# Startup, pooling-group and normalization steps of a one-core hybrid decoder step reordered between ScalarE, VectorE and GpSimd

## The chip, the cores and the metric

The kernel runs on one core of a Trainium2 chip. The metric is the device time in microseconds (us) of one execution, lower is better. Engines are named as in the profile: PE is TensorE (matmul), PEld its weight loads, DVE is VectorE, ACT is ScalarE, POOL is GpSimd and SP is SyncE, which issues most DMAs here.

## The reference

One inference step of one decoder layer on 288 token columns: a prompt of 256 positions and 8 sequences of 4 new tokens. All arithmetic is float32.

```
h    = RMSNorm(x) * g1
proj = h @ w_in + b_in                       # 2048 -> 1024 (a), 1024 (gate), 1024 (z)
u    = a * sigmoid(gate)
c    = silu(LayerNorm(depthwise_causal_conv(u, 31 taps)))
d    = mean of z over the last w positions - z      # w = 2, 4, 8, 16, one w per 256 columns
p    = (d @ pool_w) * pool_scale             # 256x256 for each of the four groups
x   += concat(c, p) @ w_out                  # 2048 -> 2048
x   += relu(RMSNorm(x) * g2 @ w_ff1)^2 @ w_ff2      # 2048 -> 8192 -> 2048
y    = RMSNorm(x) * gf
```

The kernel also returns the newest 30 columns of u and the newest 15 of z as states.

## The kernel before

**Layout.** Channels lie on the 128 partitions and the 288 tokens in the free dimension. Each product of float32 operands is made as three fp32r matmuls of 128x288: the weight's high part times the operand's high part, weight low times operand high, weight high times operand low. So each piece of 128x1024 weights that arrives by DMA in a raw buffer (`wr`, six of them) has to be split into `whi`, a cast on ACT (L274), and `wlo`, a subtraction: on DVE (way "V", L279), on POOL in two halves (way "G", L282), or by ACT and an accumulating DMA (way "D", L276 and L277). There are five buffers each for `whi` and `wlo`. A table `WAYS` gives the ways by stage, in turn.

**Order of the stages.** The first product makes the first two pairs of the input projection (conv channels 0 and 1, four PSUM banks) in eight pairs of k tiles, as the weights and the activations `xT` arrive. Then a written list, `SEQUENCE`, sets the rest of the first half: c2, c3, c4, p3, c5, p2, P3, c6, p1, P2, p0, P1, c7, P0. Here `c` and a number is a conv pair (two banks `ac`, then scaling, gate, 31 taps on ACT, DVE and POOL), small `p` is the input product of a pooling group (`pool_group`) and capital `P` the 256x256 product of that group's differences (`pool_products`, bank `pp`). The numbers in tile names count instances, so `dx3` and `pp3` are the third pooling group to come, whose window is 4 wide, and `ac12` is the product p0, `ac13` the product c7. After that come eight products of w_out with the pooling half, with the LayerNorm's mean, sums and rows between them (`BETWEEN`), eight with the conv half, the feed-forward part in four chunks, and the final norm with the output.

**What sets the order of instructions.** A scheduler writes one fixed order for each engine from priorities (the order in the code, moved by `later`) and from what it takes to be ready. The helper `mm` chains the matmuls of the first half in the order of the code, up to the stage P1: there `chain.clear()` lets the matmuls of P1, c7 and P0 go wherever the scheduler puts them. `issue_after` forces one instruction behind another on its engine's queue. On the chip each queue runs in that fixed order and waits with semaphores.

**A pooling group.** DVE scales the bank into `tz` (L483), ACT adds the bias into `z_all` (L486, L487), POOL makes windowed sums `s` by doubling (L492: two instructions per doubling), divides the sums of the first positions by their own counts (L496, `rcnt`), scales the sums of the new tokens (L499) and makes their difference (L500). DVE makes the difference `d` of the prompt (L497). ACT casts `d` to the high part of `dx` (L502) and DVE makes the low part (L503). Then PE can multiply.

**Start and end.** Nine fp32 matmuls on constants (`warm`, two PE records each) run before data arrives. The first k pair's operand `hx` is made on DVE and ACT from `xT` and the first norm's factors (`vec`). RMSNorm's row factor is applied after the first product, from a sum of squares made meanwhile (`squares`, L418). Row factors come from a square root on ACT, a reciprocal on DVE and one Newton step.

Of the kernel before, what the change touches and what calls it, by code (L numbers as in the profile page):

```python
# [16 lines left out]
P = 128  # L17
D = 2048
# [54 lines left out]
WAYS = {"c2": "GVGV", "c3": "GDGG", "c4": "GDGD", "p3": "GDDG", "c5": "GDGD", "c": "GGGV", "p": "GVVG", "w0": "VV", "w": "GG", "ff": "VV"}  # L73
# [13 lines left out]
def trunk_kernel(ctx: ExitStack, tc: tile.TileContext, io):  # L87
# [119 lines left out]
    def load_table(func, src):  # L207

        return nc.scalar.activation(few[: src.shape[0], :], src, func)

    load_table(AF.Sqrt, ones[:, 0:1])
    warm = ms("warm")
    for j in range(9):
# [17 lines left out]
    def inverse_root(mean, root, y, out):  # L231

        nc.vector.reciprocal(y, root)
        nc.vector.scalar_tensor_tensor(out=root, in0=mean, scalar=EPS, in1=y, op0=ALU.add, op1=ALU.mult)
        nc.vector.scalar_tensor_tensor(out=root, in0=root, scalar=-0.5, in1=y, op0=ALU.mult, op1=ALU.mult)
        nc.vector.scalar_tensor_tensor(out=out, in0=root, scalar=1.5, in1=y, op0=ALU.add, op1=ALU.mult)

    def rsqrt_sums(parts, scale, after=None):
# [4 lines left out]
        pt = pq[:, 0, :]  # L243
        for n, t in enumerate(parts):
            for j in range(3):
                last = mm(pt[:TB, j : j + 1], t[:, j * TB : (j + 1) * TB], ones[:, 0:1], start=n + j == 0, stop=n == len(parts) - 1 and j == 2)
        st = const.tile([TB, 12], F32, name=nm("st"))
        s = [st[:, 3 * j : 3 * j + 3] for j in range(4)]
# [17 lines left out]
    turns = {}  # L266

    def split_part(raw, src, hi, lo, way):
# [9 lines left out]
        elif way == "V":  # L278
            nc.vector.tensor_tensor(lo, raw, f32(hi), op=ALU.subtract)  # L279
# [77 lines left out]
    hx, firsts = [], []  # L357

    def first_split(k0):
# [5 lines left out]
        for k in range(k0, k0 + 2):  # L365
            if k == 0:
                nc.vector.tensor_scalar(hx[k][0], xT[:, k, :], v("norm1_g", k), None, op0=ALU.mult)  # L367
            else:
                nc.scalar.activation(hx[k][0], xT[:, k, :], AF.Copy, scale=v("norm1_g", k))  # L369
        for b in blocks[1:]:  # L370
            nc.scalar.copy(hi[:, b], raw[:, b])
        for b in blocks:
            nc.vector.tensor_tensor(lo[:, b], raw[:, b], f32(hi[:, b]), op=ALU.subtract)
# [37 lines left out]
    def squares():  # L411

        nc.scalar.copy(scratch[:, :, :, 0:1], f32(firsts[2][0])[:, 1, 1, 0:10].rearrange("p (n k t) -> p n k t", n=5, t=1))
        for q in range(8):
# [3 lines left out]
            nc.scalar.activation(dst, xq, AF.Square)  # L418
# [365 lines left out]
```

## Time and profile before

| what | value |
|---|---|
| median of 3 runs | 1084.99 us (1084.27 to 1086.06) |
| the profiled execution: time, span | 1084.57 us, 1082.8 us |
| granted PE clock, mean | 0.997 |
| PE busy | 1071.5 us, 99% |
| DVE busy | 635.4 us, 59% |
| ACT busy | 479.0 us, 44% |
| POOL busy | 173.6 us, 16% |
| DMA | 190.71 MB, mean 176 GB/s |

The span counts from the first to the last thing recorded, and 1.8 us of the execution lie outside it. A matmul's duration (292 ns) overlaps the next one's, so the pace is read from starts. "x4" in a row means that four like instructions stand together, and the start is that of the first. Idle time in brackets stands with what ended it.

### The profile page before, as it was taken

How to read it: one execution, taken by the hardware profiler on the slowest of the kernel's cores; microseconds unless marked ns; L12 is line 12 of the kernel's file. 1: busy time of each engine (PE TensorE's matmuls, PEld its weight loads, DVE VectorE, ACT ScalarE, POOL GpSimd, SP SyncE). 2: the span in 40 equal slices, each digit the busy share in tenths (PEclk: the TensorE clock that was granted, in tenths of full speed). 3: DMA queues.
4: the chain of work that ended last, by engine and by line, in shares of the span. 5: the costliest groups of instructions: out<-in, count | busy, mean ns of one | idle time of the engine just before them, and what ended most of it. 6: DMA issues, size and time to landing. Idle time of an engine off the chain costs nothing.

```text
span 1082.8 us, 19572 instructions
## 1 busy us (share of the span) xinstructions
PE 1071.5 (99%) x8198; PEld 1069.9 (99%) x8198; DVE 635.4 (59%) x818; ACT 479.0 (44%) x585; POOL 173.6 (16%) x180
## 2 busy tenths in 40 slices
PE   9999999999999999999999999999999999999996
PEld 9999999999999999999999999999999999999996
DVE  8899999678655544445544444545544445554553
ACT  8654445475544433334443333444433334444441
POOL 0878979512000000000000000000000000000001
PEclk9999999999999999999999999999999999999998
DMA  9896468545555555555555555555555555555522
GB/s 325 281 273 185 137 196 239 176 152 177 173 164 170 172 166 169 174 164 169 171 168 168 175 165 169 174 167 167 174 165 168 174 169 165 173 166 168 173 78 88
DMA packets 58296, 190.71 MB, mean 176 GB/s; under 512 B 6240, under 2 KB 11232, under 8 KB 58208
## 3 DMA queue, kind: packets, MB, share of 16 engines
q1 hardware_dynamic: 56336, 184.35, 53.9%
q0 software_dynamic: 1008, 3.67, 1.9%
q8 instruction: 64, 1.05, 0.4%
q10 hardware_dynamic: 864, 1.44, 0.4%
q14 instruction: 24, 0.20, 0.1%
HBM read 185.16 MB, written 4.28 MB: 175 GB/s over the span
## 4 chain that ended last, share of the span: by engine, by line
PE 77%; issue 20%; ACT 1%; DVE 0%; DMA 0%; POOL 0%; POOLq 0%
PE ac L305 77%; PE pp L305 1%; DMA wr<-in_w 0%; ACT whi L274 0%; POOL xT L720 0%; ACT n L595 0%; DVE wlo L279 0%; PE pt L305 0%; PE pmean L305 0%; POOLq L770 0%; DVE xT L695 0%; DVE n L592 0%; ACT whi L364 0%; ACT mx L597 0%; DVE hx L367 0%
## 5 line engine op out<-in xcount | busy, mean ns | idle before, releaser
L274 ACT CAST whi<-wr 128x1024 fp32r<-128x1024 f32 (+1 forms) x332 | 348.0, 1049 | 551.4 <-PE ac L305 533.5
L279 DVE TENSOR_TENSOR wlo<-wr,whi 128x1024 fp32r<-128x1024 f32 x288 | 353.1, 1226 | 348.5 <-ACT whi L274 348.5
L305 PE MATMUL ac<-ax,whi 128*128 128x288 f32 x2048 | 351.0, 292 | 0.0
L305 PE MATMUL ac<-fx,whi 128*128 128x288 f32 x2048 | 350.2, 292 | 0.0
L305 PEld LDWEIGHTS ac<-ax,whi 128*128 128x128 f32 x2048 | 296.0, 187 | 0.0
L305 PEld LDWEIGHTS ac<-fx,whi 128*128 128x128 f32 x2048 | 295.6, 187 | 0.0
L305 PE MATMUL ac<-ax,wlo 128*128 128x288 f32 x1024 | 217.4, 292 | 0.0
L305 PE MATMUL ac<-fx,wlo 128*128 128x288 f32 x1024 | 216.4, 292 | 0.0
L305 PEld LDWEIGHTS ac<-ax,wlo 128*128 128x128 f32 x1024 | 162.6, 187 | 0.0
L305 PEld LDWEIGHTS ac<-fx,wlo 128*128 128x128 f32 x1024 | 162.3, 187 | 0.0
L305 PE MATMUL ac<-hx,whi 128*128 128x288 f32 x768 | 131.8, 295 | 1.2 <-DVE hx L367 1.2
L720 POOL TENSOR_TENSOR xT<-xT,rf 128x288 f32<-128x288 f32 x4 | 3.1, 795 | 800.1 <-ACT rf L724 800.1
L305 PEld LDWEIGHTS ac<-hx,whi 128*128 128x128 f32 x768 | 112.1, 190 | 1.4 <-ACT hx L369 1.4
L282 POOL TENSOR_TENSOR wlo<-wr,whi 128x512 fp32r<-128x512 f32 x74 | 100.3, 1410 | 35.3 <-ACT whi L274 34.3
L461 DVE SCALAR_TENSOR_TENSOR pc<-u_all,vec,pc 128x256 f32<-128x256 f32 x232 | 99.5, 483 | 1.9 <-ACT pc L458 0.7
L305 PE MATMUL ac<-hx,wlo 128*128 128x288 f32 x384 | 80.1, 294 | 0.0
L305 PEld LDWEIGHTS ac<-hx,wlo 128*128 128x128 f32 x384 | 61.1, 190 | 0.0
L305 PE MATMUL ac<-dx,whi 128*128 128x288 f32 x256 | 46.0, 296 | 0.0
L305 PE MATMUL ac<-mx,whi 128*128 128x288 f32 x256 | 45.1, 294 | 0.1
L664 DVE SCALAR_TENSOR_TENSOR t<-ac,r 128x576 f32<-128x576 f32 x32 | 24.2, 758 | 25.1 <-PE ac L305 25.1
L305 PEld LDWEIGHTS ac<-dx,whi 128*128 128x128 f32 x256 | 38.0, 188 | 0.2
L305 PEld LDWEIGHTS ac<-mx,whi 128*128 128x128 f32 x256 | 37.5, 188 | 0.6 <-ACT mx L597 0.4
(133 smaller groups left out, 533.6 us busy)
## 6 DMA issues: line engine op xcount, KB each, us to landing
wr<-in_w SPq DMA_DIRECT2D x335, 512.0 KB, 3.8
wlo<-in_w POOLq DMA_DIRECT2D x7, 512.0 KB, 7.7
xT<-in_xT SPq DMA_DIRECT2D x8, 288.0 KB, 7.3
wr<-in_w SPq DMA_DIRECT2D x5, 256.0 KB, 3.6
out_u_out<-u_all SPq DMA_DIRECT2D x1, 1208.0 KB, 9.3
u_all<-in_hist_c SPq DMA_DIRECT2D x8, 136.0 KB, 6.2
out_z_out<-z_all SPq DMA_DIRECT2D x1, 668.0 KB, 9.9
z_all<-in_hist_p SPq DMA_DIRECT2D x4, 152.0 KB, 7.5
```

What stands on the lines that cost most here:

```text
L274: nc.scalar.copy(hi, raw)
L279: nc.vector.tensor_tensor(lo, raw, f32(hi), op=ALU.subtract)
L282: nc.gpsimd.tensor_tensor(lo[:, j : j + 2, :], raw[:, j : j + 2, :], f32(hi[:, j : j + 2, :]), op=ALU.subtract)
L305: last = nc.tensor.matmul(*args, **kw)
L461: nc.vector.scalar_tensor_tensor(out=dst, in0=up[:, w : w + SEQ], scalar=cwv[:, w : w + 1], in1=pc, op0=ALU.mult, op1=ALU.add)
L664: nc.vector.scalar_tensor_tensor(out=t, in0=bk[:, :, :T], scalar=0.0, in1=both(rows2[0]), op0=ALU.max, op1=ALU.mult)
L720: eng.tensor_tensor(xk, xk, r[:, None, :].to_broadcast([P, n, T]), op=ALU.mult)
```

## The change

Six parts.

- **Start.** The DMA of the first norm's factors moves from the front of SP's queue to ACT's queue, behind the first weight block. There are 15 warm matmuls in place of 9. On DVE the first `hx` stands ahead of the first weight split; on ACT both weight blocks of the first pair are cast ahead of the second `hx`. The squares are tied one by one behind the pairs' activations.
- **First row factors.** DVE in place of ACT copies them (`rb`) and scales the four banks at once behind that. The fourth low part of stage c2 (way "L") is made behind this.
- **Inverse roots.** ACT reads the mean square from PSUM with the function Abs_reciprocal_sqrt, and three DVE instructions follow; the reciprocal on DVE, and for the row sums two more instructions, go. This is for the first norm, the LayerNorm, the feed-forward norms and the last norm.
- **Ways of the splits.** c2, c3, c4, c7 and p0 get tables of their own. A way "V" split whose code comes after a pooling group is tied behind that group's DVE difference (`behind_pool`).
- **Pooling groups and conv sums.** POOL's three steps on the first and newest columns stand in the code ahead of DVE's difference. For the last two groups they get a higher priority, as do the scaling and gates of the first two conv pairs and the steps of the LayerNorm. The last additions into the channel sums `sum_c` move to the last conv pair, behind its product `prd`.
- **LayerNorm rows and end.** The rows are spread one k pair earlier; the silu pieces are ordered behind the casts; the first output's parts are (1,1,1,1,2,3,3) tiles in place of (1,1,2,2,3,3).

```diff
-WAYS = {"c2": "GVGV", "c3": "GDGG", "c4": "GDGD", "p3": "GDDG", "c5": "GDGD", "c": "GGGV", "p": "GVVG", "w0": "VV", "w": "GG", "ff": "VV"}
+WAYS = {"c2": "GVGL", "c3": "GVGG", "c4": "GVGD", "p3": "GDDG", "c5": "GDGD", "c7": "GGGG", "c": "GGGV", "p0": "GVGG", "p": "GVVG", "w0": "VV", "w": "GG", "ff": "VV"}
...
             first_weights(k, nc.scalar, slice(0, 1))
+            nc.scalar.dma_start(vec[:, 0:NG], io["vec"][:, 0:NG])
             first_weights(k, nc.sync, slice(1, 2))
-    nc.sync.dma_start(vec[:, 0:NG], io["vec"][:, 0:NG])
...
-    for j in range(9):
+    for j in range(15):
         nc.tensor.matmul(warm[:, 0, 0:P], ones, ones, start=True, stop=True)
...
-    def inverse_root(mean, root, y, out):
-        nc.vector.reciprocal(y, root)
-        nc.vector.scalar_tensor_tensor(out=root, in0=mean, scalar=EPS, in1=y, op0=ALU.add, op1=ALU.mult)
-        nc.vector.scalar_tensor_tensor(out=root, in0=root, scalar=-0.5, in1=y, op0=ALU.mult, op1=ALU.mult)
-        nc.vector.scalar_tensor_tensor(out=out, in0=root, scalar=1.5, in1=y, op0=ALU.add, op1=ALU.mult)
+    def inverse_root(mean, y, t, out, after=None):
+        nc.scalar.activation(y, mean, AF.Abs_reciprocal_sqrt, bias=eps[: y.shape[0], :])
+        if after is not None:
+            load_table(after, y[:, 0:1])
+        nc.vector.scalar_tensor_tensor(out=t, in0=mean, scalar=EPS, in1=y, op0=ALU.add, op1=ALU.mult)
+        nc.vector.scalar_tensor_tensor(out=t, in0=t, scalar=-0.5, in1=y, op0=ALU.mult, op1=ALU.mult)
+        nc.vector.scalar_tensor_tensor(out=out, in0=t, scalar=1.5, in1=y, op0=ALU.add, op1=ALU.mult)
...
-        nc.vector.tensor_scalar(s[0], pt[:TB, 0:3], scale * DC, EPS, op0=ALU.mult, op1=ALU.add)
-        nc.scalar.activation(s[1], s[0], AF.Sqrt)
-        if after is not None:
-            load_table(after, s[1][:, 0:1])
-        nc.vector.reciprocal(s[2], s[1])
-        nc.vector.tensor_tensor(s[3], s[2], s[2], op=ALU.mult)
-        nc.vector.scalar_tensor_tensor(out=s[3], in0=s[3], scalar=-0.5, in1=s[0], op0=ALU.mult, op1=ALU.mult)
-        nc.vector.scalar_tensor_tensor(out=s[2], in0=s[3], scalar=1.5, in1=s[2], op0=ALU.add, op1=ALU.mult)
-        return s[2], pq[:, 1, :T], last
+        inverse_root(mean, st[:, 0:3], t, st[:, 4:7], after=after)
+        return st[:, 4:7], pq[:, 1, :T], last
...
         elif way == "V":
-            nc.vector.tensor_tensor(lo, raw, f32(hi), op=ALU.subtract)
+            with tc.issue_after(behind_pool[0]) if behind_pool else nullcontext():
+                nc.vector.tensor_tensor(lo, raw, f32(hi), op=ALU.subtract)
+        elif way == "L":
+            late.append((lo, raw, f32(hi)))
...
-            if i == N8 - 2:
-                for part in (sum_c[:, 1, :], c):
-                    nc.gpsimd.tensor_tensor(sum_c[:, 0, :], sum_c[:, 0, :], part, op=ALU.add)
+            if i == N8 - 1:
+                for part in (sum_c[:, 1, :], cs[i // 2][:, 0, :]):
+                    with tc.issue_after(multiplied.ins):
+                        nc.gpsimd.tensor_tensor(sum_c[:, 0, :], sum_c[:, 0, :], part, op=ALU.add)
...
-        first_sums = s[:, :, PH : PH + w - 1]
-        nc.gpsimd.tensor_tensor(first_sums, first_sums, rcnt[:, None, w - 2 : 2 * w - 3].to_broadcast([P, 2, w - 1]), op=ALU.mult)
-        nc.vector.scalar_tensor_tensor(out=d[:, :, 0:SEQ], in0=s[:, :, PH:ZO], scalar=1.0 / w, in1=z[:, :, PH:ZO], op0=ALU.mult, op1=ALU.subtract)
-        news = [x[:, :, ZO:ZL].rearrange("p m (b t) -> p m b t", t=ZS)[:, :, :, PH:] for x in (s, z)]
-        nc.gpsimd.tensor_scalar(news[0], news[0], 1.0 / w, None, op0=ALU.mult)
-        nc.gpsimd.tensor_tensor(d[:, :, SEQ:T].rearrange("p m (b t) -> p m b t", t=NS), news[0], news[1], op=ALU.subtract)
-        dh, dl = act2("dx", tag="p", bufs=4)
-        nc.scalar.copy(dh, d)
-        nc.vector.tensor_tensor(dl, d, f32(dh), op=ALU.subtract)
+        with later(-LATER if g < 2 else 0):
+            first_sums = s[:, :, PH : PH + w - 1]
+            nc.gpsimd.tensor_tensor(first_sums, first_sums, rcnt[:, None, w - 2 : 2 * w - 3].to_broadcast([P, 2, w - 1]), op=ALU.mult)
+            news = [x[:, :, ZO:ZL].rearrange("p m (b t) -> p m b t", t=ZS)[:, :, :, PH:] for x in (s, z)]
+            nc.gpsimd.tensor_scalar(news[0], news[0], 1.0 / w, None, op0=ALU.mult)
+            nc.gpsimd.tensor_tensor(d[:, :, SEQ:T].rearrange("p m (b t) -> p m b t", t=NS), news[0], news[1], op=ALU.subtract)
+            pooled = nc.vector.scalar_tensor_tensor(out=d[:, :, 0:SEQ], in0=s[:, :, PH:ZO], scalar=1.0 / w, in1=z[:, :, PH:ZO], op0=ALU.mult, op1=ALU.subtract)
+            dh, dl = act2("dx", tag="p", bufs=4)
+            nc.scalar.copy(dh, d)
+            nc.vector.tensor_tensor(dl, d, f32(dh), op=ALU.subtract)
         dd[g] = dh, dl
+        behind_pool[:] = [pooled.ins]
...
-        nc.scalar.copy(rb, pr)
+            nc.vector.tensor_copy(rb, pr)
+            for b in (pair0[1], pair0[0], pair1[1], pair1[0]):
+                scaled = nc.vector.tensor_tensor(b[:, :T], b[:, :T], rb, op=ALU.mult)
+        with tc.issue_after(scaled.ins):
+            nc.vector.tensor_tensor(*late.pop(), op=ALU.subtract)
...
-    BETWEEN = {5: {4: ln_mean}, 6: {6: ln_sums}, 7: {2: ln_rows}}
+    BETWEEN = {5: {4: ln_mean}, 6: {6: ln_sums}, 7: {0: ln_rows}}
...
-    root, first, s_f = [cst[:TB, 2 + 3 * j : 5 + 3 * j] for j in range(3)]
-    nc.scalar.activation(root, sums_f, AF.Sqrt, bias=eps[:TB, :])
-    inverse_root(sums_f, root, first, s_f)
+    s_f = cst[:TB, 6:9]
+    inverse_root(sums_f, cst[:TB, 2:5], ends[:TB, 0, 4:7], s_f)
...
-    finish(nc.vector, rows_f, ((0, 1), (1, 1), (2, 2), (4, 2), (6, 3), (9, 3)))
+    finish(nc.vector, rows_f, ((0, 1), (1, 1), (2, 1), (3, 1), (4, 2), (6, 3), (9, 3)))
```

Three places show what this does to the queues. First PE, from the beginning of product p0 (`ac12`), where the twelve matmuls of the product P2 have just ended; `whi43` and `wlo43` to `whi47` are the weights in their order of arrival, 47 the small pooling block and 48 the first of c7. Before:

```order
L305 MATMUL ac12_1924<-hx2_177,whi43_1897 128x288 x2
L305 MATMUL ac12_1924<-hx2_177,wlo43_1898 128x288 x2
L305 MATMUL ac12_1924<-hx2_177,whi43_1897 128x288 x4
L305 MATMUL ac12_1924<-hx2_177,wlo43_1898 128x288 x2
L305 MATMUL ac12_1924<-hx2_177,whi43_1897 128x288 x2
L305 MATMUL ac12_1924<-hx3_188,whi44_1902 128x288 x2
L305 MATMUL ac12_1924<-hx3_188,wlo44_1903 128x288 x2
L305 MATMUL ac12_1924<-hx3_188,whi44_1902 128x288 x4
```

And after, from the last rows on `whi43`:

```order
L303 MATMUL ac12_1924<-hx2_183,whi43_1896 128x288 x4
L303 MATMUL ac12_1924<-hx2_183,wlo43_1897 128x288 x2
L303 MATMUL ac12_1924<-hx2_183,whi43_1896 128x288 x2
L303 MATMUL ac12_1924<-hx3_194,whi44_1901 128x288 x2
L303 MATMUL ac13_2090<-hx1_172,whi48_2061 128x288 x2
L303 MATMUL pp3_2044<-dx3_1876,whi47_2023 128x288 x2
L303 MATMUL ac12_1924<-hx3_194,wlo44_1902 128x288 x2
L303 MATMUL ac12_1924<-hx3_194,whi44_1901 128x288 x4
```

Two matmuls of c7 and two of the third pooling product now stand in the middle of p0, 26 matmuls into it, ahead of the first use of `wlo44`. Before, the first matmul on `dx3` stood some sixty rows further on, in c7.

Second DVE, around the second pooling group's difference `d2` and the split of `wlo37`, the last of the four blocks of c6 (`wlo39` to `wlo41` belong to p1). Before, with `wlo37` fourteen rows above the first of these:

```order
L279 TENSOR_TENSOR wlo40_1703<-wr40_1698,whi40_1702 128x1024
L461 SCALAR_TENSOR_TENSOR pc3_1061<-u_all_87,vec_85,pc3_1061 128x256 x6
L445 TENSOR_TENSOR ac10_1588<-ac10_1588,rb1_247 128x288
L461 SCALAR_TENSOR_TENSOR pc3_1061<-u_all_87,vec_85,pc3_1061 128x256
L445 TENSOR_TENSOR ac10_1588<-ac10_1588,rb1_247 128x288
L279 TENSOR_TENSOR wlo42_1857<-wr42_1854,whi42_1856 128x512
L461 SCALAR_TENSOR_TENSOR pc3_1061<-u_all_87,vec_85,pc3_1061 128x256
L497 SCALAR_TENSOR_TENSOR d2_1535<-s7_1532,z_all_91 128x2x256
```

And after:

```order
L462 SCALAR_TENSOR_TENSOR c2_724<-u_all_87,vec_85,pc2_725 128x256
L462 SCALAR_TENSOR_TENSOR pc3_1062<-u_all_87,vec_85,pc3_1062 128x256 x5
L503 SCALAR_TENSOR_TENSOR d2_1536<-s7_1533,z_all_91 128x2x256
L275 TENSOR_TENSOR wlo37_1581<-wr37_1573,whi37_1580 128x1024
L275 TENSOR_TENSOR wlo39_1696<-wr39_1688,whi39_1695 128x1024
L275 TENSOR_TENSOR wlo40_1704<-wr40_1699,whi40_1703 128x1024
```

The split of `wlo37` moved from far ahead of `d2` to just behind it; the same holds for `wlo30` behind `d1`, and for `wlo44` behind `d3`. Between the third group's `tz3` and its `d3` the DVE queue now holds fourteen rows of conv taps (`pc`) and the two low parts of `dx2`.

Third POOL, at the third pooling group (`s8`, `s9`, `d3`). Before:

```order
L492 TENSOR_TENSOR s8_1866<-z_all_91 128x422 x2
L469 TENSOR_TENSOR sum_c_248<-sum_c_248,c3_1060 128x288
L492 TENSOR_TENSOR s9_1869<-s8_1866 128x420 x2
L282 TENSOR_TENSOR wlo48_2062<-wr48_2057,whi48_2061 128x512 x2
L282 TENSOR_TENSOR wlo49_2067<-wr49_2059,whi49_2066 128x512 x2
L496 TENSOR_TENSOR s9_1869<-s9_1869,rcnt_131 128x2x3
L282 TENSOR_TENSOR wlo50_2076<-wr50_2071,whi50_2075 128x512 x2
L499 TENSOR_SCALAR s9_1869<-s9_1869 128x2x8x4
L492 TENSOR_TENSOR s10_2033<-z_all_91 128x422 x2
L500 TENSOR_TENSOR d3_1872<-s9_1869,z_all_91 128x2x32
```

And after:

```order
L470 TENSOR_TENSOR sum_c_254<-sum_c_254,c3_1061 128x288
L494 TENSOR_TENSOR s8_1865<-z_all_91 128x422 x2
L494 TENSOR_TENSOR s9_1868<-s8_1865 128x420 x2
L499 TENSOR_TENSOR s9_1868<-s9_1868,rcnt_137 128x2x3
L501 TENSOR_SCALAR s9_1868<-s9_1868 128x2x8x4
L502 TENSOR_TENSOR d3_1871<-s9_1868,z_all_91 128x2x32
L280 TENSOR_TENSOR wlo45_1910<-wr45_1905,whi45_1909 128x512 x2
L280 TENSOR_TENSOR wlo46_1915<-wr46_1907,whi46_1914 128x512 x2
L280 TENSOR_TENSOR wlo48_2062<-wr48_2057,whi48_2061 128x512 x2
```

The chain of the group now runs through on POOL without weight splits in it, and the splits stand behind it.

More of the change, by code (lines that the diff above doesn't have):

```diff
@@ L264, in spread @@
         return pr, last
-    turns = {}
+    turns, late = {}, []
+    behind_pool = []
     def split_part(raw, src, hi, lo, way):
@@ L372, in first_split @@
         for b in blocks:
-            nc.vector.tensor_tensor(lo[:, b], raw[:, b], f32(hi[:, b]), op=ALU.subtract)
+            with tc.issue_after(first.ins) if k0 == 0 else nullcontext():
+                nc.vector.tensor_tensor(lo[:, b], raw[:, b], f32(hi[:, b]), op=ALU.subtract)
         for k in (k0 + 1, k0):
@@ L547, in trunk_kernel @@
             pool_products(i)
-    load_table(AF.Sqrt, f32(mixp[1][0])[:, 0:1])
+    load_table(AF.Abs_reciprocal_sqrt, f32(mixp[1][0])[:, 0:1])
     with later(2 * LATER):
```

81 lines of the change are left out of this document (43 added, 38 removed).

## The prediction

> **What bounds the kernel now.** I read the page first, then PE's waits, then the timeline of the four places that the change touches. These are the page's row of busy times, all of PE's waits with their totals, and one stretch of the windows view (us, busy time and instructions of each engine).
>
> ```profile
> PE 1071.5 (99%) x8198; PEld 1069.9 (99%) x8198; DVE 635.4 (59%) x818; ACT 479.0 (44%) x585; POOL 173.6 (16%) x180
> ...
> PE ac L305 <- DVE hx L367: 1.2, 1, 1.2
> PE warm L214 <- DVE cst L229: 1.0, 1, 1.0
> PE ends L712 <- DVE cst L236: 0.2, 1, 0.2
> ...
> 40.00:160.00 120.00, 120.00 (x924) 120.00 (x924) 114.94 (x246) 62.83 (x88) 103.88 (x87) 1.00 0.70 199
> ```
>
> PE is the bound nearly everywhere. Its 924 matmuls in 120 us make one each 0.130 us, and I use that as the pace. So a gain can only come from places where PE is off this pace, and any wait that the change puts into PE's fixed order adds in full. DVE's 114.94 of 120 us is the warning: here DVE has only 4% left, and this is where its order is changed.
>
> **The start.** PE, DVE and ACT in the first 11 us, the stretch after the first real matmul, and the DMA of the factors (`vec`, issue to landing at the end of the row):
>
> ```profile
> 1.04 4.21 PE L214 MATMUL warm<-ones 128*128 128x128 f32 x18 [1.04 <-DVE cst L229]
> 6.40 1.30 PE L305 MATMUL ac<-hx,whi 128*128 128x288 f32 x4 [1.15 <-DVE hx L367]
> 6.40:10.60 4.20, 4.20 (x18) 4.20 (x18) 3.43 (x7) 3.37 (x7) 0.00 (x0) 1.00 1.05 408
> ...
> 5.28 0.69 DVE L373 TENSOR_TENSOR wlo<-wr,whi 128x512 fp32r<-128x512 f32 x1 [2.88 <-ACT whi L364]
> 5.89 0.36 DVE L367 TENSOR_SCALAR hx<-xT,vec 128x288 fp32r<-128x288 f32 x1
> ...
> 5.59 0.54 ACT L369 ACTIVATE hx<-xT,vec 128x288 fp32r<-128x288 f32 x1 [0.35 <-DMA xT<-in_xT]
> 8.82 0.62 ACT L364 CAST whi<-wr 128x512 fp32r<-128x512 f32 x1 [0.33 <-DMA wr<-in_w]
> ...
> vec<-in_vec SPq DMA_DIRECT2D x1, 8.0 KB, 3.1
> ```
>
> The first 18 real matmuls took 4.20 us where 18 x 0.130 are 2.34: 1.86 us are lost to half pace, after a gap of 1.15 us. Measured at full pace, the real work of before starts at 6.40 + 1.86 = 8.26. After, 30 warm records follow each other from 1.04. At half pace one takes about 4.21/18, less the last one's drain: 0.22 us, so all 30 at half pace end at 7.6. The trace does not show when an unbroken run is let go; 4.21 us of it were not enough. If full pace comes right there, at 5.25, the last 11 cost 0.11 each and real work starts at 6.45; if it never comes before the end, at 7.6. The gain is 1.8 or 0.7; a floor for the start is `hx`: without the split at 5.28 ahead of it, DVE begins at 5.6 when `xT` is there (ACT's row of 5.59) and PE could start at 6.1, gain 2.1. I take 1.8, since the 4.20 us of real work from 6.40 needed just such a stretch. The data keep up: the second k pair is wanted at 6.45 + 24 x 0.130 = 9.6, its first block is cast from 8.82 to 9.44, its second in as long again, by 10.0, and wanted four matmuls later, at 10.1. `vec` behind the 256 KB block on ACT's queue is the unknown: issued 0.4 later, with 3.1 us to land, it arrives near 4.3, and up to 1.3 us more would still hide behind `xT`. SP's queue starts its first `xT` 0.45 us sooner; ACT's table load moves by as much and lies in its 2 us wait for the first block.
>
> The Trainium skill, "TensorE: Matmul & The Clock Gate" (What's actually happening), has the clock released after a busy window of 3.4 us that runs freely, so the release point varies with the phase. By that the release is an estimate between 4.5 and 7.9, and real work starts between 6.1 and 7.6: the same two ends.
>
> **Pooling group three in p0.** This is the main loss. In before the rows of PE, DVE, POOL and ACT around it are these, with groups of DVE's instructions from 138 to 151.5 us (busy sum, mean ns):
>
> ```profile
> 136.54 0.42 PE L305 MATMUL pp<-dx,whi 128*128 128x288 f32 x2
> 141.74 0.42 PE L305 MATMUL ac<-hx,whi 128*128 128x288 f32 x2
> ...
> 137.65 0.74 DVE L483 TENSOR_TENSOR tz<-ac,rb 128x576 f32<-128x576 f32 x1
> 151.92 1.33 DVE L497 SCALAR_TENSOR_TENSOR d<-s,z_all 128x512 f32<-128x512 f32 x1
> 161.11 0.69 DVE L497 SCALAR_TENSOR_TENSOR d<-s,z_all 128x512 f32<-128x512 f32 x1
> 133.03 1.21 DVE L279 TENSOR_TENSOR wlo<-wr,whi 128x1024 fp32r<-128x1024 f32 x1
> ...
> L461 DVE SCALAR_TENSOR_TENSOR pc<-u_all,vec,pc 128x256 f32<-128x256 f32 x25 | 10.0, 476 | 0.0
> L466 DVE TENSOR_REDUCE c<-prd 128x32 f32<-128x1024 f32 x1 | 1.2, 1206 | 0.0
> L515 DVE SCALAR_TENSOR_TENSOR dx<-pp,vec,dx 128x288 fp32r<-128x288 f32 x2 | 1.0, 504 | 0.0
> ...
> 140.42 1.74 POOL L492 TENSOR_TENSOR s<-z_all 128x422 f32<-128x422 f32 x2
> 142.88 2.19 POOL L492 TENSOR_TENSOR s<-s 128x420 f32<-128x420 f32 x2
> 150.02 0.20 POOL L496 TENSOR_TENSOR s<-s,rcnt 128x6 f32<-128x6 f32 x1
> 150.18 2.53 POOL L282 TENSOR_TENSOR wlo<-wr,whi 128x512 fp32r<-128x512 f32 x2
> 153.35 0.38 POOL L499 TENSOR_SCALAR s<-s 128x64 f32<-128x64 f32 x1 [0.64 <-DVE d L497]
> 105.06 0.34 POOL L500 TENSOR_TENSOR d<-s,z_all 128x64 f32<-128x64 f32 x1
> ...
> 139.46 0.31 ACT L487 ACTIVATE z_all<-tz,vec 128x32 f32<-128x32 f32 x1
> 157.27 0.68 ACT L502 CAST dx<-d 128x576 fp32r<-128x576 f32 x1 [2.61 <-POOL d L500]
> ```
>
> Product p1 has issued its last matmul when P2's (`pp`) begin at 136.54. In the new order PE then has 12 + 24 + 2 + 2 = 40 matmuls, 5.2 us, and comes to `pp3<-dx3` at 141.74. Two suppliers stand in the way. (a) DVE's queue: `tz3` at 137.65 (0.66 to the next start), fourteen taps of 0.40, two low parts of 0.50 at most, `d3` 0.69, then ACT's cast 0.68: 137.65 + 0.66 + 5.6 + 1.0 + 0.69 + 0.68 = 146.3. (b) POOL's chain from the end of `z` at 139.77: 1.74 + 2.19 + 0.20 + 0.38 + 0.34, 144.6, and `d3` and the cast behind it, 146.0. Both come to PE 4.2 to 4.5 us late. The cast of `whi48` ahead of it, 1.05 us after the last matmul on `whi43`, falls inside this wait. Then `wlo44`, tied behind `d3`, ends 1.2 us after it, 0.3 us after the two `pp3` matmuls. Sum 4.7. It rises to 5.9 if the reduction of 1.2 us, which now stands ahead of `tz3`, still holds DVE when p1 ends, and is 3.8 if POOL's four sums go at 0.85 and DVE is early. I take 5.0: DVE has been busy all along at 137.65, so part of the reduction counts.
>
> The row of 151.92 speaks for the upper half: `d` took 1.33 us while POOL was splitting a weight (150.18 to 152.71), 0.69 us at 161.11. After, POOL begins to split `wlo45` just as `d3` becomes free to run. The Trainium skill, "SBUF — State Buffer" (Who interferes with whom), says that a DVE instruction with two SBUF inputs contends with a GpSimd instruction that reads SBUF, and that the later one blocks fully. The trace agrees in that one row; by the rule `d3` alone would add 0.6 and my total would be 1088.8.
>
> **Groups one and two.** PE's first use of `wlo37` and of `wlo30`, and POOL's rows of the sums ahead of them:
>
> ```profile
> 121.20 0.42 PE L305 MATMUL ac<-hx,wlo 128*128 128x288 f32 x2
> 100.92 0.42 PE L305 MATMUL ac<-hx,wlo 128*128 128x288 f32 x2
> ...
> 113.01 2.72 POOL L492 TENSOR_TENSOR s<-z_all 128x422 f32<-128x422 f32 x2
> 121.93 0.80 POOL L469 TENSOR_TENSOR sum_c<-c,c 128x288 f32<-128x288 f32 x1
> 91.55 6.55 POOL L492 TENSOR_TENSOR s<-s 128x420 f32<-128x420 f32 x6
> ```
>
> For `wlo37`: sums from 113.01, six of them at 0.87 to 1.09 (the last row's pace), then `sum_c` 0.80, counts, scaling and difference 0.92, `d2` 0.69, the split 1.21: between 121.9 and 123.2, wanted at 121.20: 0.7 to 2.0 late, less up to 0.3 since starts follow 0.04 to 0.08 before the recorded ends. I take 1.1. For `wlo30`: 98.10 + 0.97 + 0.69 + 1.21 = 100.97 against 100.92, so 0.1 (0 to 0.7 with a slow `d1`).
>
> **LayerNorm and end.** PE where the conv half of w_out starts, and DVE at the last norm:
>
> ```profile
> 219.00 0.43 PE L305 MATMUL ac<-dx,whi 128*128 128x288 f32 x2
> 219.55 0.54 PE L305 MATMUL ac<-mx,whi 128*128 128x288 f32 x2
> 221.85 0.43 PE L305 MATMUL ac<-mx,whi 128*128 128x288 f32 x2
> ...
> 1071.57 0.17 DVE L233 RECIPROCAL cst<-cst 96x3 f32<-96x3 f32 x1 [1.53 <-ACT cst L708]
> 1071.85 0.16 DVE L234 SCALAR_TENSOR_TENSOR cst<-ends,cst 96x3 f32<-96x3 f32 x1
> ```
>
> From 219.00 to 221.85 PE issues 2 + 14 matmuls, 2.08 us at pace, in 2.85: 0.77 lost to late `mx`. Rows spread 24 matmuls earlier (3.1 us) and a shorter chain should win most of it; the silu pieces' new order only permutes ACT. I take 0.6 (0 to 0.77). At the end nothing covers the chain: the reciprocal's 0.28 goes, and one small output part more costs less than it brings forward; 0.3 (0.1 to 0.5).
>
> The rest I cost at nothing: the reciprocals of the feed-forward norms lie beside PE's chunks, the ways' moves and `rb` on DVE lie in windows where PE has no gap; the later `sum_c` steps must be there for the LayerNorm's mean, 40 us on. If DVE's cover of 5 us in 120 is gone, each such step costs its length; I leave 1 us for it in the range.
>
> **Sum.** Losses 5.0 + 1.1 + 0.1 = 6.2, gains 1.8 + 0.6 + 0.3 = 2.7, net +3.5 on the profiled 1084.57, which lies 0.42 under the median: 1088.1.
>
> **Rivals.**
> - *The third group is in time* (faster). If `d3` runs ahead of the taps, or PE's order hides it, only the gains and 1.2 us of loss stay: 1084.57 - 2.7 + 1.2 = 1083.1, or 1081.9 without these too. It decides at `d3` done by 141.0 in before's clock, 4.6 us sooner than worked out. Against it: both suppliers reach the same time independently.
> - *Half the wait* (same). The DVE queue ahead is shorter, POOL undisturbed, and the wait is 2 to 3 us: 1085 to 1086.5.
> - *The long wait cools PE* (slower still). A gap of 1.15 us at 6.40 was followed by half pace, but PE had not been let go before it, so the trace does not show a re-cooling. If 4 us idle bring it, 1.9 us come on top: 1090.0. The same page of the Trainium skill on the clock gate (What's actually happening) has the clock fall back after an idle window of 3.4 us; two matmuls of c7 split the wait, and the longer piece is near 4 us.
> - *The warm matmuls end cold*: the start brings 0.7, 1089.2. Inside the range.
>
> **Chances.** The forecast 0.57 (1086.5 to 1089.5), cooled 0.10, half 0.14, in time 0.19. What a measurement of this kernel can tell from no change is about 0.2%, 2.2 us. Above 1087.2 lie most of the forecast and the cooled case: 0.60. Within 2.2 us lie the half wait and the forecast's lower end: 0.21. Faster 0.19. The range goes from 1082.2, in the case without the third wait, to 1090.3.
>
> **What the profile would show.** After: PE's waits list `pp` waiting for ACT's `dx` near 140 us with 3 to 5 us, and `ac` for `wlo` near 120 with about 1; warm records at two paces and no slow matmul behind them; no gap at the first `mx`. I am wrong if PE runs through p0 without a gap, if the slow matmuls at the start remain, or if a wait appears in c2, whose fourth low part is made late.

## The result, and the profile after

The changed kernel takes 1097.35 us (median of 4, 1096.26 to 1098.25) against 1085.12 us for the kernel before in the same comparison. The ratio is 1.0112, 95% interval 1.0095 to 1.0130: slower by 12 us, 1.1%, clear of the noise; the forecast of 1088.1 stood 3 above before. The profiled execution took 1096.26 us, its span is 1094.4. Of all executions behind this document one was in a slower state, 2426 us in the version with fifteen warm matmuls and nothing else, and the ratios leave it out.

The page's busy times and the clock granted in 40 slices, then all of PE's waits that are not the opening one:

```profile
PE 1075.8 (98%) x8210; PEld 1073.8 (98%) x8210; DVE 638.4 (58%) x814; ACT 474.5 (43%) x581; POOL 175.0 (16%) x182
PEclk9999989999999999999999999999999999999998
...
PE pp L303 <- ACT dx L505: 3.9, 1, 3.9
PE ac L303 <- DVE wlo L275: 3.3, 3, 2.1
PE ac L303 <- ACT whi L269: 1.0, 1, 1.0
PE ac L303 <- DVE hx L365: 0.4, 1, 0.4
```

The waits stand where they were forecast, 8.2 us of them behind the start, and a slice with a lower granted clock appears, which before did not have in the middle of the run. The windows view of the two main places (the number behind the engines' busy times is the granted clock), and PE's rows there:

```profile
121.00:124.00 3.00, 0.91 (x7) 0.67 (x6) 3.00 (x3) 1.62 (x2) 2.93 (x2) 1.00 0.00 0
124.00:128.50 4.50, 4.50 (x24) 4.50 (x24) 4.50 (x4) 0.50 (x1) 2.77 (x2) 0.62 0.83 289
145.00:152.50 7.50, 1.97 (x9) 1.16 (x7) 7.50 (x14) 1.72 (x2) 7.34 (x9) 0.75 0.00 1
152.50:156.00 3.50, 3.49 (x15) 3.49 (x16) 3.50 (x5) 0.00 (x0) 3.50 (x3) 0.55 0.68 187
...
100.32 0.53 PE L303 MATMUL ac<-hx,wlo 128*128 128x288 f32 x2 [0.60 <-DVE wlo L275]
123.46 0.53 PE L303 MATMUL ac<-hx,wlo 128*128 128x288 f32 x2 [2.09 <-DVE wlo L275]
125.80 1.16 PE L303 MATMUL ac<-hx,whi 128*128 128x288 f32 x4
...
146.60 0.53 PE L303 MATMUL ac<-hx,whi 128*128 128x288 f32 x2 [1.01 <-ACT whi L269]
151.06 0.85 PE L303 MATMUL pp<-dx,whi 128*128 128x288 f32 x2 [3.93 <-ACT dx L505]
152.51 0.85 PE L303 MATMUL ac<-hx,wlo 128*128 128x288 f32 x2 [0.61 <-DVE wlo L275]
```

At 100.32 PE has waited for `wlo30`, at 123.46 for `wlo37`, at 146.60 to 152.51 for c7's weights, `dx3` and `wlo44` in turn. Behind the last two places PE works, but at a granted clock of 0.62 and 0.55 over the stretch: four matmuls take 1.16 us from first start to last end there, 0.68 elsewhere. DVE and POOL in front of these waits:

```profile
97.91 1.23 DVE L503 SCALAR_TENSOR_TENSOR d<-s,z_all 128x512 f32<-128x512 f32 x1
119.95 1.24 DVE L503 SCALAR_TENSOR_TENSOR d<-s,z_all 128x512 f32<-128x512 f32 x1
121.11 6.74 DVE L275 TENSOR_TENSOR wlo<-wr,whi 128x1024 fp32r<-128x1024 f32 x3
148.93 1.32 DVE L503 SCALAR_TENSOR_TENSOR d<-s,z_all 128x512 f32<-128x512 f32 x1
150.17 3.96 DVE L275 TENSOR_TENSOR wlo<-wr,whi 128x1024 fp32r<-128x1024 f32 x2
...
119.35 7.42 POOL L280 TENSOR_TENSOR wlo<-wr,whi 128x512 fp32r<-128x512 f32 x4
148.44 8.60 POOL L280 TENSOR_TENSOR wlo<-wr,whi 128x512 fp32r<-128x512 f32 x5
```

Three splits took 6.74 us on DVE, 2.3 each, and four halves 7.42 on POOL. Both engines were subtracting weights at the same time.

The first matmul behind the feed-forward part (`ends`) starts at 1069.38 us before and at 1081.02 after, 11.64 later. Comparing the starts of the same matmuls in both traces says where these came from. A minus is a gain.

| stretch, from and to | before, us | after, us | difference |
|---|---|---|---|
| start to the spread of the first row factors (`pt`) | 0 to 35.74 | 0 to 34.48 | -1.26 |
| to the first pooling product (`wlo30` in it) | to 110.02 | to 109.73 | +0.97 |
| to P2's product (`wlo37` in it) | to 136.54 | to 140.49 | +4.24 |
| to the LayerNorm's mean (p0 in it) | to 201.15 | to 213.47 | +8.37 |
| to the first feed-forward matmul | to 270.31 | to 281.95 | -0.68 |
| feed-forward | to 1069.38 | to 1081.02 | 0.00 |
| end | to the end | to the end | about 0 |

In the p0 stretch the first use of `wlo44` comes 6.56 us late: without a wait it would have started at 145.95, 2 + 2 matmuls behind the 26 of p0, and it starts at 152.51. The 14 matmuls from there take 3.36 us where 14 x 0.130 are 1.82, another 1.54.

### The profile page after: what moved, and what is told of

It reads as the page before. It is cut to its first block, busy times and chain, and to the rows that moved or that the text cites. A ratio compares the mean times of both kernels' runs of the same rounds, so it can differ in the third digit from the quotient of the medians.

```text
span 1094.4 us, 19595 instructions
## 1 busy us (share of the span) xinstructions
PE 1075.8 (98%) x8210; PEld 1073.8 (98%) x8210; DVE 638.4 (58%) x814; ACT 474.5 (43%) x581; POOL 175.0 (16%) x182
## 4 chain that ended last, share of the span: by engine, by line
PE 74%; issue 20%; DVE 5%; DMA 0%; POOL 0%; POOLq 0%; ACTq 0%; DVEq 0%
PE ac L303 73%; DVE pc L462 3%; DVE wlo L275 1%; DMA vec<-in_vec 0%; DVE d L503 0%; PE pp L303 0%; POOL xT L731 0%; DVE c L467 0%; PE pt L303 0%; DVE dx L519 0%; DVE ac L446 0%; DVE tz L485 0%; DVE c L462 0%; DVE u_all L450 0%; PE pmean L303 0%
## 5 line engine op out<-in xcount | busy, mean ns | idle before, releaser
L275 DVE TENSOR_TENSOR wlo<-wr,whi 128x1024 fp32r<-128x1024 f32 (+1 forms) x287 | 356.9, 1245 | 349.3 <-ACT whi L269 349.2
L280 POOL TENSOR_TENSOR wlo<-wr,whi 128x512 fp32r<-128x512 f32 x78 | 107.5, 1407 | 34.2 <-ACT whi L269 33.6
```

Of the source, the lines that this page charges most:

```text
L280: nc.gpsimd.tensor_tensor(lo[:, j : j + 2, :], raw[:, j : j + 2, :], f32(hi[:, j : j + 2, :]), op=ALU.subtract)
```

## The experiments

The theory (A): the tie of DVE's splits behind the pooling differences makes three weights late; POOL's and DVE's simultaneous splits lengthen this; the idle PE then loses its full clock. The rivals: PE's own order, with matmuls of c7 and P1 inside p0 (B); or causes other than contention and idleness for the long splits and the slow matmuls. No version leaves anything out; those with constant matmuls, gaps or a second subtraction add work.

**Without the tie.**

```diff
-        behind_pool[:] = [pooled.ins]
```

> The changed kernel, but a low part made on DVE is no longer tied behind the pooling group's difference. Theory A (the tie makes wlo30, wlo37 and wlo44 late; everything else follows from these waits): PE's waits at 100, 123 and 146 to 152 us and the slow matmuls behind them go, 12.8 us of 1097.35: 1083.5 to 1085.5. Theory B (POOL's new order, or matmuls of c7 and of the third pooling product standing inside p0, make the waits): most of the loss stays, 1092 or more.

Measured 1085.28 us, ratio to before 1.0008 (0.9999 to 1.0018). The loss of 12 us is gone but for 0.8, which the interval does not tell from nothing. Its waits behind the start:

```profile
PE ac L303 <- DVE wlo L275: 1.1, 1, 1.1
PE pp L303 <- DVE dx L506: 0.9, 1, 0.9
```

These two, at 159 and 166 us, are new and small; they eat the gains of the other parts: this version is 1.2 us ahead of before at P2's product (135.36 against 136.54) and 1.4 behind at the LayerNorm's mean (202.52 against 201.15).

**Before with the tie alone.**

```diff
-            nc.vector.tensor_tensor(lo, raw, f32(hi), op=ALU.subtract)
+            with tc.issue_after(behind_pool[0]) if behind_pool else nullcontext():
+                nc.vector.tensor_tensor(lo, raw, f32(hi), op=ALU.subtract)
...
+        behind_pool[:] = [pooled.ins]
```

> The kernel before with nothing but the tie: a low part made on DVE goes behind the last pooling group's difference. Theory A: this alone brings the waits in p0 and at the last block of c6, with the slow matmuls: 1089 to 1097. Theory B (it takes POOL's new order or the new ways): 1084 to 1086.

Measured 1093.68 us, ratio 1.0076 (1.0061 to 1.0091). The tie alone costs 9 of the 12 us, with POOL's order and the ways as before; so it is sufficient for most of the loss, and by the run above nearly all of the loss needs it. The profiled execution, 1091.41 us, is the fastest of the four. PE's rows at the start, at `wlo37` and at `wlo44`:

```profile
6.58 0.77 PE L307 MATMUL ac<-hx,whi 128*128 128x288 f32 x4 [1.65 <-DVE hx L369]
121.92 0.54 PE L307 MATMUL ac<-hx,wlo 128*128 128x288 f32 x2 [1.21 <-DVE wlo L281]
146.62 0.53 PE L307 MATMUL ac<-hx,wlo 128*128 128x288 f32 x2 [2.11 <-DVE wlo L281]
```

Behind the wait of 1.21 us no slow matmul follows, behind that of 2.11 some do. In the changed kernel the wait for `wlo37` is 2.09 and has slow matmuls behind it, so the 3 us that the other edits add lie at least in part there; they were not taken apart further.

The first row has a use of its own: with nine warm matmuls and an idle time of 1.65 us, this execution ran its first real matmuls at full pace (0.77 us for four, where the profiled execution of before took 1.30).

**PE's order put right.** The matmuls of P1 and c7 stay chained in the order of the code.

```diff
-        if (kind, i) == ("P", 1):
+        if (kind, i) == ("P", 0):
             chain.clear()
```

> The changed kernel with the matmuls of P1 and c7 chained in the order of the code, so that none of them stands inside p0. Theory A: PE meets the late wlo44 at the same place, the wait only loses the two matmuls and the ScalarE cast in front of it: 1095.5 to 1098. Theory B (the order on PE makes the wait in p0): the 8.1 us lost there go, 1089 to 1090.

Measured 1097.21 us, ratio 1.0115 (1.0100 to 1.0130). Theory B falls: PE now meets the late `wlo44` itself, in one wait.

```profile
152.34 0.85 PE L303 MATMUL ac<-hx,wlo 128*128 128x288 f32 x2 [7.49 <-DVE wlo L275]
```

**Fewer splits on POOL beside DVE's.**

```diff
-WAYS = {... "p0": "GVGG", "p": "GVVG", ...}
+WAYS = {... "p0": "GVDD", "p": "DVVD", ...}
```

> The changed kernel, but the low parts that POOL made right behind the pooling groups' steps in p1, p2 and half of those in p0 come from ScalarE and an accumulating DMA, so POOL reads no weights while DVE makes the tied ones. If the two engines slow each other: the tied splits beside it go from 2.29 to about 1.23 us and the differences from 1.24 to 0.69, the wait for wlo37 from 2.1 to about 0.6 and that in p0 by 1.5 or more, and some of the slow matmuls go: 1091 to 1094.5. If the long splits have another cause: 1096 to 1099 (ScalarE has 1.05 us more for each of these blocks).

Measured 1091.87 us, ratio 1.0068 (1.0051 to 1.0085). At `wlo37`, where POOL now issues DMAs in place of subtractions:

```profile
120.32 0.69 DVE L503 SCALAR_TENSOR_TENSOR d<-s,z_all 128x512 f32<-128x512 f32 x1
120.92 3.49 DVE L275 TENSOR_TENSOR wlo<-wr,whi 128x1024 fp32r<-128x1024 f32 x3
...
122.20 0.53 PE L303 MATMUL ac<-hx,wlo 128*128 128x288 f32 x2 [0.87 <-DVE wlo L275]
```

The difference takes 0.69 us in place of 1.24 and the three splits 3.49 in place of 6.74; the wait is 0.87, and no slow matmuls follow. In p0 this version is no clean test: POOL still splits a block of c7 there, and the scheduler moved more of c7 ahead of `wlo44`. Two waits of 1.00 and 1.19 us are left there within 2.7 us, and slow matmuls follow them.

**The two engines side by side, elsewhere.** In the third feed-forward chunk of before, each low part is also subtracted on POOL into a scratch tile.

```diff
             nc.vector.tensor_tensor(lo, raw, f32(hi), op=ALU.subtract)
+            if beside:
+                for j in range(0, 4, 2):
+                    nc.gpsimd.tensor_tensor(scr, raw[:, j : j + 2, :], f32(hi[:, j : j + 2, :]), op=ALU.subtract)
```

> The kernel before, with each low part of the third feed-forward chunk also computed on GpSimd into a scratch tile, from the same cast on, so that the two engines subtract at the same time from the same tiles. If they slow each other: VectorE's 128x1024 split takes 1.7 to 2.4 us there, against 1.225 in the chunks beside it. If the 2.3 us at 121 us had another cause: 1.225 everywhere. The time stays within 1 us of before either way, since these splits have some 2 us to spare.

The groups of DVE's and POOL's instructions from 700 to 860 us, and DVE's group of the feed-forward part in the changed kernel, where POOL is idle:

```profile
L279 DVE TENSOR_TENSOR wlo<-wr,whi 128x1024 fp32r<-128x1024 f32 x47 | 89.2, 1900 | 52.2 <-ACT whi L274 51.7
...
L283 POOL TENSOR_TENSOR scr<-wr,whi 128x512 f32<-128x512 f32 x90 | 162.4, 1842 | 0.0
```
```profile
L275 DVE TENSOR_TENSOR wlo<-wr,whi 128x1024 fp32r<-128x1024 f32 x193 | 236.4, 1225 | 270.2 <-ACT whi L269 270.2
```

A split is 1.900 us on the mean there against 1.225 alone (1.225 too in the chunk of this run from 500 to 600 us). So the contention is shown apart from this change. It is not the same for each split: they take from 1.22 to 2.32, and POOL's halves from 1.27 to 2.29. My guess about the time was a miss: 1101.01 us, 16 above before. POOL's two halves hold a raw block for 2 x 1.84 = 3.7 us, and PE uses a block in 24 x 0.130 = 3.1, so POOL, busy all the time from 700 to 860 us, had become the bound of that chunk.

**Filling the waits.** Constant matmuls ahead of c6 and p0 in the changed kernel, work that PE does where it would have been idle.

```diff
+        for _ in range(busy):
+            mm(banks[0][:, 384:512], ones, ones, start=True, stop=True)
...
+        gemm(each(bk), hx, busy=0 if g else 22)
...
+            conv_pair(i, conv_products(i, classes=TURN if i == 5 else "", busy=9 if i == 6 else 0))
```

> The changed kernel with 9 constant fp32 matmuls ahead of c6 and 22 ahead of p0, 1.9 and 4.7 us of TensorE work that fills the waits but moves nothing else forward. If the idle time brings the half pace behind the waits: the slow matmuls behind 124 and 151 us go, 3.2 us, less at most 1 us by which the filling overshoots: 1094 to 1095.5. If the slow matmuls come from something else (the late operands, the busy VectorE): 1097 or more.

Measured 1095.10 us, ratio to before 1.0095 (1.0080 to 1.0110): more work, and 2.25 us less than the changed kernel's 1097.35. At `wlo37` the slow matmuls are gone (four take 0.70), in p0 two short waits are left and slow matmuls follow:

```profile
123.51 0.54 PE L303 MATMUL ac<-hx,wlo 128*128 128x288 f32 x2
125.47 0.70 PE L303 MATMUL ac<-hx,whi 128*128 128x288 f32 x4
...
150.25 0.53 PE L303 MATMUL pp<-dx,whi 128*128 128x288 f32 x2 [0.79 <-ACT dx L507]
151.70 0.53 PE L303 MATMUL ac<-hx,wlo 128*128 128x288 f32 x2 [0.92 <-DVE wlo L275]
152.07 1.09 PE L303 MATMUL ac<-hx,whi 128*128 128x288 f32 x4
```

**Idle time alone.** Six gaps in the feed-forward part of before, each a matmul that waits for a chain of ACT and POOL instructions on constants; no weight is late there.

```diff
+    def gap(n):
...
+        mm(pq[:, 0, :T], ones, xT[:, 0, :], start=True, stop=True)
+        nc.scalar.copy(a[0], pq[:, 0, :T])
+        for j in range(n):
+            nc.gpsimd.tensor_tensor(a[1 - j % 2], a[j % 2], a[j % 2], op=ALU.add)
+        return mm(pq[:, 1, :T], ones, a[n % 2], start=True, stop=True)
```

> The kernel before with six gaps put into TensorE's work in the feed-forward part, 50 us apart, where nothing else is late: a constant product, a ScalarE copy of it and 0, 1, 2, 3, 4 and 6 GpSimd additions of about 0.8 us in a chain, and a matmul that waits for the last. If idle time alone brings the half pace: no slow matmuls behind the gaps of about 1 us, a spell of 14 to 28 matmuls at 0.24 us behind the longest ones (over 3.4 us by the page's window in the Trainium skill, TensorE: Matmul & The Clock Gate, What's actually happening), and either behind those between. If the half pace had to do with late operands or VectorE: no slow matmuls anywhere.

The kernel took 1136.75 us with its gaps. PE's rows at three of them and the windows behind them:

```profile
540.50 0.75 PE L305 MATMUL gap<-gp,ones 128*128 128x288 f32 x2 [0.95 <-ACT gp L656]
633.75 0.75 PE L305 MATMUL gap<-gp,ones 128*128 128x288 f32 x2 [2.43 <-POOL gp L658]
851.01 1.32 PE L305 MATMUL gap<-gp,ones 128*128 128x288 f32 x2 [3.91 <-POOL gp L658]
```
```profile
540.40:542.40 2.00, 1.90 (x12) 1.80 (x13) 1.00 (x1) 0.04 (x1) 0.00 (x0) 1.00 0.45 164
633.70:634.90 1.20, 1.15 (x7) 1.04 (x8) 0.00 (x0) 0.00 (x0) 0.00 (x0) 1.00 0.38 102
634.90:638.50 3.60, 3.60 (x18) 3.60 (x17) 0.00 (x0) 0.00 (x0) 0.00 (x0) 0.53 0.31 112
851.00:856.90 5.90, 5.89 (x22) 5.60 (x23) 0.00 (x0) 0.00 (x0) 0.00 (x0) 0.50 0.12 44
```

Behind 0.95 us idle the clock stays at 1.00. Behind 2.43 it stays for 1.2 us more, then is 0.53 over 3.6 us. Behind 3.91 it is at half from the first matmul on, for 5.9 us. The gaps of 3.17, 4.66 and 6.14 us were all followed by half pace from the first matmul on too. Idle time is enough: no weight is late here, and DVE has nothing to do in the two slow windows.

**The start.** The first factors (`vec`) back at the front of SP's queue, in the changed kernel.

```diff
-            nc.scalar.dma_start(vec[:, 0:NG], io["vec"][:, 0:NG])
...
+    nc.sync.dma_start(vec[:, 0:NG], io["vec"][:, 0:NG])
```

> The changed kernel with the DMA of the first factors at the front of SP's queue again. If their landing at 6.50 us sets the start: the first real matmul goes from 7.11 to about 6.4 us, PE's wait for hx goes, and the time falls by 0.5 to 1.0: 1096.4 to 1096.9. If the weights or the activations set it: no change, 1097.3.

Measured 1097.72 us, ratio to before 1.0114 (1.0100 to 1.0128): no gain over 1097.35. In the changed kernel the factors had landed late; now PE begins at 6.63 but waits for the second weight block instead. First two rows of the changed kernel, then two of this one:

```profile
6.60 0.37 DVE L365 TENSOR_SCALAR hx<-xT,vec 128x288 fp32r<-128x288 f32 x1 [4.20 <-DMA vec<-in_vec]
7.11 1.03 PE L303 MATMUL ac<-hx,whi 128*128 128x288 f32 x6 [0.37 <-DVE hx L365]
```
```profile
6.63 0.78 PE L303 MATMUL ac<-hx,whi 128*128 128x288 f32 x4
8.30 1.32 PE L303 MATMUL ac<-hx,whi 128*128 128x288 f32 x8 [0.36 <-ACT whi L370]
```

**The rest by itself.** Two versions keep the warm matmuls and the order of the start, the inverse roots, the LayerNorm rows and the end: the changed kernel without the tie and with `vec` on SP's queue, and the same with POOL's order, the sums and the ways of before too. The first edit below is against the changed kernel, the second is the core of what is added to it.

```diff
-        behind_pool[:] = [pooled.ins]
...
-            nc.scalar.dma_start(vec[:, 0:NG], io["vec"][:, 0:NG])
...
+    nc.sync.dma_start(vec[:, 0:NG], io["vec"][:, 0:NG])
```

> The changed kernel without the tie and with the first factors on SP's queue. The untied version's 1085.28 less the 0.7 to 1.0 us of its late start: 1084.3 to 1084.6. If the tie was needed to bring the third pooling group in time, its wait of 0.9 us at 159 us stays.

```diff
-WAYS = {"c2": "GVGL", "c3": "GVGG", "c4": "GVGD", "p3": "GDDG", "c5": "GDGD", "c7": "GGGG", "c": "GGGV", "p0": "GVGG", "p": "GVVG", "w0": "VV", "w": "GG", "ff": "VV"}
+WAYS = {"c2": "GVGL", "c3": "GDGG", "c4": "GDGD", "p3": "GDDG", "c5": "GDGD", "c": "GGGV", "p": "GVVG", "w0": "VV", "w": "GG", "ff": "VV"}
...
-            if i == N8 - 1:
-                for part in (sum_c[:, 1, :], cs[i // 2][:, 0, :]):
-                    with tc.issue_after(multiplied.ins):
+            if i == N8 - 2:
+                for part in (sum_c[:, 1, :], c):
+                    with nullcontext():
...
+            pooled = nc.vector.scalar_tensor_tensor(out=d[:, :, 0:SEQ], in0=s[:, :, PH:ZO], scalar=1.0 / w, in1=z[:, :, PH:ZO], op0=ALU.mult, op1=ALU.subtract)
             news = [x[:, :, ZO:ZL].rearrange("p m (b t) -> p m b t", t=ZS)[:, :, :, PH:] for x in (s, z)]
...
-            pooled = nc.vector.scalar_tensor_tensor(out=d[:, :, 0:SEQ], in0=s[:, :, PH:ZO], scalar=1.0 / w, in1=z[:, :, PH:ZO], op0=ALU.mult, op1=ALU.subtract)
```

> The changed kernel with all of the pooling part undone: no tie, GpSimd's steps behind VectorE's difference, channel sums and ways as before (but for c2's late part), first factors on SP's queue. What is left is the start, the inverse roots, the LayerNorm rows and the end. If these gain what their rows show (1.7 to 1.9 at the start, 0.7 at the LayerNorm, 0 at the end): 1082.0 to 1082.6, faster than both. If the gains are given back: 1084 to 1085.

Measured 1085.68 us, ratio 1.0007 (0.9998 to 1.0016), and 1085.57 us, ratio 1.0003 (0.9994 to 1.0012). The first landed above its range and kept its 0.9 us wait. The second was a clear miss of the 1082.0 to 1082.6: it is 0.4 us ahead of before when P2 starts (136.14 against 136.54), and 1.5 behind at the LayerNorm's mean (202.65 against 201.15). In between PE waits for low parts from DVE and for `dx3` around 160 to 170 us. What in the remaining edits (row factors on DVE, the late part of c2, the priorities) brings these was not tested.

**Two parts put into the kernel before.** Fifteen warm matmuls and nothing else; and these with the inverse roots and the LayerNorm's rows and silu order of the changed kernel, all else as before.

```diff
-    for j in range(9):
+    for j in range(15):
```

> The kernel before with 15 warm matmuls and no other edit. The profiled execution of before paid 1.9 us for a cold start, another one nearly nothing, so the mean gain is about half of it, less what the longer warm row delays the first product: 1084.0 to 1084.7. If the cold start is paid in most executions: 1083.1 to 1083.6.

The second, against the kernel before, has the line above and these, among others of the same parts:

```diff
-    load_table(AF.Sqrt, ones[:, 0:1])
+    load_table(AF.Abs_reciprocal_sqrt, ones[:, 0:1])
...
-        nc.vector.reciprocal(y, root)
+        nc.scalar.activation(y, mean, AF.Abs_reciprocal_sqrt, bias=eps[: y.shape[0], :])
...
+        with later(-LATER):
+            norm["rows"], last = spread(norm["sums"])
...
-    BETWEEN = {5: {4: ln_mean}, 6: {6: ln_sums}, 7: {2: ln_rows}}
+    BETWEEN = {5: {4: ln_mean}, 6: {6: ln_sums}, 7: {0: ln_rows}}
...
-            nc.scalar.activation(n[:, m, :], n[:, m, :], AF.Silu, bias=v("ln_b", i), scale=v("ln_g", i))
+            with tc.issue_after(copied) if j else nullcontext():
+                nc.scalar.activation(n[:, m, :], n[:, m, :], AF.Silu, bias=v("ln_b", i), scale=v("ln_g", i))
```

> The kernel before with 15 warm matmuls, the inverse roots of the changed kernel and its LayerNorm rows and silu order; pooling, ways, first factors and output parts as before. The LayerNorm's 0.7 us on top of the start's 0.3 to 1: 1083.2 to 1084.0, faster than both kernels. If the new orders cost something in the c7 to P0 stretch as in the version without the pooling part: 1084.5 to 1085.5.

Measured 1084.39 us, ratio 0.9997 (0.9988 to 1.0006), no difference that can be told; and 1083.35 us, ratio 0.9987 (0.9979 to 0.9996). The second beats before by 1.4 us in the same comparison, with an interval that just leaves out no change, and the changed kernel by 14. Its only waits of PE behind the opening one are in the first microseconds:

```profile
PE ac L299 <- DVE hx L361: 0.5, 1, 0.5
PE ac L299 <- DVE wlo L367: 0.2, 1, 0.2
PE ac L299 <- ACT whi L358: 0.2, 1, 0.2
```

## Why the prediction was right in its places and wrong in its sizes

The direction, all three places of loss and the LayerNorm's gain came out. The sum did not: +3.5 was forecast, +11.6 measured between the two profiled executions. By its terms:

| term | forecast | measured | what made the difference |
|---|---|---|---|
| start | -1.8 | -1.26 | `vec` landed 5.3 us after its issue, not 3.1; with it early the second weight block was late |
| `wlo30` | +0.1 | +0.97 | `d1` took 1.23 us, not 0.69 |
| `wlo37` | +1.1 | +4.24 | `d2` and the split beside POOL; then slow matmuls |
| p0 | +5.0 | +8.37 | `d3` and `wlo44` beside POOL; then slow matmuls |
| LayerNorm | -0.6 | -0.68 | as forecast |
| end | -0.3 | 0 | the reciprocal's time came back in the output |

**The splits' duration is the term that failed first.** The step took 0.69 us for a difference and 1.21 for a split, though the changed order puts POOL's splits right beside them, already running. Measured 1.24 and 2.3 at `wlo37` (+0.55 and +1.09), 1.32 and 2.29 in p0 (+0.63 and +1.08). The difference's 0.69 came from a row, 161.11, where POOL stood idle. The split's 1.21 at 133.03 is the more treacherous: POOL was splitting there too, in the first row below. The second of its two halves began at 133.04, 0.01 us behind DVE's split, and it was this half that was long, 2.35 us in place of 1.27. The same trace has a split that started behind POOL's sums, and it took 1.69. From before:

```profile
131.28 4.11 POOL L282 TENSOR_TENSOR wlo<-wr,whi 128x512 fp32r<-128x512 f32 x2
153.68 2.72 POOL L492 TENSOR_TENSOR s<-z_all 128x422 f32<-128x422 f32 x2
153.96 1.69 DVE L279 TENSOR_TENSOR wlo<-wr,whi 128x1024 fp32r<-128x1024 f32 x1
```

The row of 1.33 us at 151.92 had been quoted, and the rule of the Trainium skill, "SBUF — State Buffer" (Who interferes with whom), had been weighed, but only for `d3`, as an extra of 0.6; it holds for every instruction with two operands in SBUF, the splits above all. The runs agree with the rule in kind (1.225 us alone, 1.900 mean and 2.3 at most beside POOL; at 133 us the later one paid). Added for both groups and `d1` it would have given 1088.1 + 3.9 = 1092.0. (With the 0.64 of the row at 151.92 alone the total is 1088.7, not the 1088.8 written.)

**The clock is the second.** It was a rival with a tenth of the chance, for p0 alone, and stood at nothing in the sum. It came at both places: 24 matmuls from the wait at 123.46 on took 4.74 us for 3.12, and 14 in p0 took 3.36 for 1.82, 3.2 us in all. The gap run shows that 2.43 us idle are enough. That is less than the idle window of 3.4 us that the Trainium skill, "TensorE: Matmul & The Clock Gate" (What's actually happening), gives. That p0's wait of 3.9 us brings it agrees with the Trainium skill there; the wait of 2.1 us brought it too, which that section does not lead one to expect.

The forecast's +3.5, with 3.9 for the splits and differences, 3.2 for the clock, and 0.8 that the start and the end failed to bring, makes 11.4 of the 11.6.

**The mechanism stood.** `d3` began 8.4 us after P2's first matmul, 140.49 to 148.93; by POOL's chain 8.1 had been worked out, by DVE's queue 8.4, and it was DVE's queue that it came behind. The rival in which the third group is in time falls with the wait of 3.93 us, and the thought that PE's order makes the wait falls with the chained version; that the tie is what costs is shown by both its removal and its addition.

**The start** was read from one execution of before, whose first 18 matmuls were slow. Of the four kept traces with nine warm matmuls three are like that (before and both runs with edits in the feed-forward part: 1.30 us for the first four), and the version with the tie alone ran them at full pace. In none of the ten with fifteen are they slow. But the longer row has a price: by itself in the kernel before it moved the first real matmul from 6.40 to 7.21 us. So fifteen were worth 0.4 us by the medians (1084.39 against 1084.79), inside the uncertainty. The windows view gives the clock as 1.00 in these first microseconds, in slow and quick starts alike, so that the slow pace there comes from the clock is not shown. The Trainium skill's words on the freely running window, in the section named above, had said that the release point varies, and the traces agree in this: the 30 records of the fifteen warm matmuls take from 4.96 us in one execution to 6.42 in another. I used them for the end of the range only.

**The end** was a wrong sum: the chain to the last row factors is 0.27 us shorter (2.80 against 3.07), but from the first output part to the end of the span it is 9.6 against 9.4 us, with one part more.

## What to carry to other kernels

Where an instruction moves to stand beside another engine's work, take its duration from several rows with that neighbour, and look which of the two started first: a row that is as short as if alone may be one in which the neighbour paid. Where PE is the bound and a wait of two microseconds or more appears, add the slow matmuls behind it, here about 1.6 us each time, to the wait. And a cold start seen in one profiled execution is no constant of the kernel: look at a second execution before counting it as a gain.

## What the runs showed of the hardware that was not expected

- A PE that had idled 2.09 us (2.43 in the gap run) ran 1.5 (1.3) us more at full clock and only then fell to half, for 3.4 us in both, read in windows of 0.2 us. Behind 3.91 us idle it was at half at once, and for 5.9 us. Single waits of 0.87, 0.95 and 1.21 us brought no half clock, but two short ones close together did: 0.79 and 0.92 us in the version with filled waits, 1.00 and 1.19 in the one with fewer splits on POOL.
- DVE's split of 1.225 us took up to 2.32 beside POOL's, and POOL's half of 1.27 us 1.84 on the mean. Two halves then are 3.7 us, and one split and two halves one after the other are 3.8, so two engines on the same kind of subtraction hardly do more side by side than one after the other. Which of them is lengthened changes: at 133 us of before it was POOL's half alone.
- An 8 KB DMA landed 5.3 to 5.6 us after its issue behind a 256 KB block on ACT's queue, in five traces, and 3.0 to 3.3 at the front of SP's, in seven.
